# One-hot tiles built one token at a time on VectorE, all low halves on VectorE, and 88 instead of 68 expert chunks prepared during routing

## The chip, the cores and the metric

The kernel runs on one core of one Trainium2 chip. The metric is the device time of one execution in microseconds (us). Engines are named as in the profile: PE is TensorE (matmuls), PEld its weight loads, DVE is VectorE, ACT is ScalarE, POOL is GpSimd, SP is SyncE, which here only issues DMAs.

## What is computed

A decoder trunk of 2 layers for one sequence of 512 tokens and width 1024. Each layer has a mixer (RWKV-7 heads and a pooling mixer) and a PEER expert layer; both are preceded by an RMSNorm with shift and scale from a conditioning vector. The change touches the expert layer most. Cut to what matters, it is:

```python
def peer_ffn(h, peer_q, peer_keys, peer_u, peer_v):        # 8 heads, 128 x 128 experts
    q = (h @ peer_q).reshape(B, S, 8, 2, 128)
    scores = einsum('bshpd,hpkd->bshpk', q, peer_keys)       # 128 keys a half
    s, i = top_k(scores, 16)
    cand_s = s[..., 0, :, None] + s[..., 1, None, :]         # 16 x 16 candidates
    cand_i = i[..., 0, :, None] * 128 + i[..., 1, None, :]
    top_s, sel = top_k(cand_s, 16)
    idx = take_along_axis(cand_i, sel); gate = softmax(top_s)
    # per token: 8 * 16 = 128 chosen experts
    act = gelu(einsum('td,ted->te', hx, peer_u[idx]))
    out = einsum('te,ted->td', gate * act, peer_v[idx])
```

## The kernel before

**Two ways to the same sum.** The 512 tokens are 4 tiles of 128. Tile 0 goes the sparse way: its 128 chosen rows of `peer_u` and of `peer_v` are fetched by indirect DMAs (`gather_load`, issued on POOL, 512 KB each for the 128 tokens) and used on DVE (`gather_use`: line 873 for a u row, line 881 for a v row). The 384 tokens of tiles 1 to 3 go the dense way: all 16384 experts in 128 chunks of 128. A chunk's *first product* (`s_chunk`) is 24 matmuls of 128x384, h times the chunk of `peer_u`. After a Gelu it is multiplied with a gate matrix G (zero where an expert was not chosen). Its *second product* (`back`) is 18 matmuls of 128x512 with the chunk of `peer_v`, summed in PSUM.

**Products in three parts.** For accuracy in fp32r every f32 operand is split in a high half (ACT rounds it: line 265 for weights, line 1156 for v) and a low half (what remains, a subtraction). The low half of a weight tile (`wsp`, 128x1024, line 266) is made on POOL for every second tile of the list `seq`, on DVE for the others (`on_pool`); some tiles of the mixer's `w_in` always go to POOL. The low halves of v (`vv`, two of 128x512 a chunk, line 1157) are made one on DVE and one on POOL.

**The stages of a layer.** (1) Mixer. (2) Queries: 16 tiles of 24 matmuls, each followed by scores and a top-16 on DVE (`score`); meanwhile pieces of the next modulation vector are summed (`ada_acc`: with `side=ND` ACT scales and POOL adds). (3) Routing: for each token tile the candidates are built, sorted and picked on DVE, with one multiply of 128x400 on POOL (lines 981 and 983). For tiles 1 to 3 the gate matrix is built by one-hots: for each of 48 blocks of `TB` = 8 tokens, `onehot` writes tiles with a 1 at (token's expert row i, column j), two of them weighted with the gate's high and low part, and `onehot_mm` turns them into G with 16 matmuls of 128x128 in f16 (a weight load and a matmul for each token and part). G goes to a DRAM scratch. In between, `s_ahead` computes the first products of the first `SPILL` chunks and stores their Gelu in DRAM. (4) Dense: for chunk c, `front` reads the stored Gelu back (c < SPILL) or computes the first product there and then, multiplies with G (line 1145) and splits the result (lines 1147, 1148); `values` splits v; `back` multiplies; `gathers` loads and uses the rows of tile 0.

**What sets the order.** Routing steps and first products are interleaved by `blend` with a weight for each step (`WC`, `WP`, `WG`, `WT`, and `WO` for a one-hot block). `upto(c)` says how many gathered rows are loaded by chunk c: 24 in routing, 0.9 a chunk up to SPILL, and the rest evenly over the chunks from SPILL to 123. The framework then schedules all instructions by estimated times and fixes each engine's order; at run time every engine works its list in that order and waits by semaphores.

## Time and profile before

| | |
|---|---|
| time, three runs | 3843.79, 3853.39, 3864.01 us (median 3853.39) |
| profiled execution, from first to last instruction | 3864.3 us |
| busy in it: PE, DVE, POOL, ACT | 3636.7 us (94%), 3061.0 (79%), 2206.7 (57%), 1494.1 (39%) |
| granted TensorE clock, mean | 0.91 of full speed |
| DMA | 810.70 MB, 210 GB/s over the span |

Busy time is the time in which at least one instruction of the engine was under way. A matmul's end is modelled, so a busy PE is not a PE at its peak. [...] The stages of layer 0 lie at 0 to 467 us (mixer), 467 to 597 (queries), 597 to 1115 (routing), 1121 to 1392 (dense, chunks whose first product was stored) and 1392 to 1920 (dense, the other 60); those of layer 1 at 1947, 2367, 2485, 3006 and 3273 us.

### The profile page before, as it was taken

What the parts mean: (1) busy time and instruction counts of PE and PEld (TensorE: products, weight loads), DVE (VectorE), ACT (ScalarE), POOL (GpSimd) and SP (SyncE); (2) the same over time, 40 slices, a digit from 0 to 9 for tenths busy, and PEclk for the clock granted to TensorE, in tenths of its full rate; (3) what the DMA queues carried; (4) which work ended last, traced back from release to release, by engine and by line L of the source; (5) the groups of instructions that cost most, each with busy time, mean ns of one, the idle gap of its engine ahead of it and who ended that gap; (6) DMA issues with size and microseconds to landing.
All of it is one profiled execution on the core that took longest, in us unless ns stands there. A gap on an engine that the chain in (4) does not pass through costs nothing. (4 is left out here: it accounts for less than half of the span.)

```text
span 3864.3 us, 51554 instructions
## 1 busy us (share of the span) xinstructions
PE 3636.7 (94%) x18154; PEld 3097.8 (80%) x18154; DVE 3061.0 (79%) x5457; ACT 1494.1 (39%) x2361; POOL 2206.7 (57%) x1440
## 2 busy tenths in 40 slices
PE   5999898899999999999998999999999999999998
PEld 4787688778788888888776877887888888888887
DVE  4765489988659999999848456999886798778888
ACT  4443263344443333333353424334344433333333
POOL 3532285656446677887627204366554566767765
PEclk7886799889789999999988789998887999999999
DMA  5223253455469999999713224245554899889885
GB/s 180 77 67 103 93 186 119 159 181 179 154 227 336 340 338 322 330 331 330 265 60 93 66 77 143 90 141 177 179 170 174 308 340 336 286 303 315 308 297 214
DMA packets 349859, 810.70 MB, mean 210 GB/s; under 512 B 45216, under 2 KB 178080, under 8 KB 346272
## 3 DMA queue, kind: packets, MB, share of 16 engines
q1 hardware_dynamic: 275872, 538.94, 41.5%
q0 software_dynamic: 73728, 268.47, 19.3%
q8 instruction: 142, 2.33, 0.2%
q14 instruction: 117, 0.96, 0.1%
HBM read 722.89 MB, written 84.41 MB: 209 GB/s over the span
## 5 line engine op out<-in xcount | busy, mean ns | idle before, releaser
L283 PE MATMUL pss<-hi,wsp 128*128 128x384 f32 (+1 forms) x5168 | 1148.0, 378 | 47.5 <-DVE wsp L266 15.7
L1174 PE MATMUL ps<-vv,wg 128*128 128x512 f32 x4608 | 1098.8, 396 | 58.9 <-ACT wg L1147 29.7
L283 PEld LDWEIGHTS pss<-hi,wsp 128*128 128x128 f32 x5168 | 1021.1, 208 | 120.4 <-DVE wsp L266 17.9
L1174 PEld LDWEIGHTS ps<-vv,wg 128*128 128x128 f32 x4608 | 867.7, 190 | 257.3 <-ACT wg L1147 38.5
L266 POOL TENSOR_TENSOR wsp<-raw,wsp 128x1024 fp32r<-128x1024 f32 x185 | 479.1, 2590 | 439.6 <-ACT wsp L265 420.3
L1157 POOL TENSOR_TENSOR vv<-raw,vv 128x512 fp32r<-128x512 f32 x256 | 387.2, 1513 | 369.5 <-ACT vv L1156 347.0
L265 ACT ACTIVATE wsp<-raw 128x1024 fp32r<-128x1024 f32 x341 | 359.8, 1057 | 587.4 <-PE pss L283 397.6
L283 PE MATMUL pss<-lo,wsp 128*128 128x384 f32 (+1 forms) x2584 | 534.9, 348 | 0.0
L283 PEld LDWEIGHTS pss<-lo,wsp 128*128 128x128 f32 x2584 | 463.7, 189 | 21.9 <-issue 0.5
L873 DVE SCALAR_TENSOR_TENSOR row<-row,hx 128x1024 f32<-128x1024 f32 x256 | 426.3, 1670 | 33.0 <-DMA row<-u,ex 32.8
L881 DVE SCALAR_TENSOR_TENSOR ox<-row,wx,ox 128x1024 f32<-128x1024 f32 x254 | 420.0, 1654 | 15.4 <-DMA row<-v,ex 11.7
L1156 ACT ACTIVATE vv<-raw 128x512 fp32r<-128x512 f32 x512 | 293.7, 621 | 255.2 <-DMA raw<-v 227.4
L1055 PE MATMUL ps<-oh,oh 128*128 128x128 f16 x1536 | 374.7, 414 | 5.5 <-DVE oh L1038 5.5
L867 POOL DMA_INDIRECT row<-v,ex x256 | 339.4, 1326 | 66.3 <-issue 47.7
L1147 ACT ACTIVATE wg<-ge 128x384 fp32r<-128x384 f32 x256 | 132.3, 522 | 617.6 <-DVE ge L1145 506.7
L867 POOL DMA_INDIRECT row<-u,ex x256 | 338.0, 1320 | 50.2 <-issue 32.5
L1036 POOL TENSOR_TENSOR oh<-oh,selg 128x1024 f16<-128x1024 f16 x96 | 208.4, 2173 | 266.2 <-PE ps L1055 252.8
L1055 PEld LDWEIGHTS <-oh 128*128 128x128 f16 x1536 | 217.1, 146 | 136.8 <-issue 9.7
L1157 DVE TENSOR_TENSOR vv<-raw,vv 128x512 fp32r<-128x512 f32 x256 | 254.1, 993 | 61.1 <-ACT vv L1156 61.0
L1145 DVE TENSOR_TENSOR ge<-ge,g 128x192 f32<-128x192 f32 x496 | 245.6, 532 | 28.1 <-DMA g<-gscr 18.3
L1057 ACT ACTIVATE gb<-ps 128x512 f32<-128x512 f32 x192 | 213.2, 1111 | 122.7 <-PE ps L1055 120.5
L266 DVE TENSOR_TENSOR wsp<-raw,wsp 128x1024 fp32r<-128x1024 f32 x156 | 219.9, 1410 | 38.0 <-ACT wsp L265 37.1
(459 smaller groups left out, 4102.8 us busy)
## 6 DMA issues: line engine op xcount, KB each, us to landing
raw<-uT SPq DMA_DIRECT2D x256, 512.0 KB
raw<-v SPq DMA_DIRECT2D x256, 512.0 KB
gscr<-gb SPq DMA_DIRECT2D x24, 2048.0 KB
g<-gscr SPq DMA_DIRECT2D x124, 384.0 KB
gespill<-ge SPq DMA_DIRECT2D x136, 192.0 KB
ge<-gespill SPq DMA_DIRECT2D x136, 192.0 KB
ada<-ada SPq DMA_DIRECT2D x96, 256.0 KB
raw<-ada SPq DMA_DIRECT2D x48, 512.0 KB
```

Source lines behind the costliest of these rows:

```text
L265: S.activation(w[:, 0], raw, AF.Copy)
L266: (G if on_pool(i) else V).tensor_tensor(w[:, 1], raw, w[:, 0].bitcast(F32), op=ALU.subtract)
L283: TE.matmul(pt, w[:, a, k * P:(k + 1) * P], hs[k][b], start=start and n == 0, stop=stop and n == len(steps) - 1)
L867: G.indirect_dma_start(out=rows[n], out_offset=None, in_=A["u" if n < P else "v"], in_offset=bass.IndirectOffsetOnAxis(ap=ex[:, n % P:n % ...
L873: V.scalar_tensor_tensor(row, row, 1.0, hx, op0=ALU.mult, op1=ALU.mult, accum_out=dots[:, e:e + 1])
L881: V.scalar_tensor_tensor(ox, row, wx[:, e:e + 1], ox, op0=ALU.mult, op1=ALU.add)
L1055: TE.matmul(pt[:, tt], oj[:, :, t4 * 4 + tt], xg[:, :, t4 * 4 + tt], start=(q == 0), stop=(q == 1))
L1057: S.activation(gb[:, :, o:o + 4].rearrange("p i t -> p t i"), pt, AF.Copy, scale=1.0 / GSC)
L1145: V.tensor_tensor(gq, gq, g[:, :, c % IG], op=ALU.mult)
L1156: S.activation(vv[0][q], raw[:, q * T:(q + 1) * T], AF.Copy)
L1157: vlo[q] = (V, G)[q].tensor_tensor(vv[1][q], raw[:, q * T:(q + 1) * T], vv[0][q].bitcast(F32), op=ALU.subtract)
L1174: end[0] = TE.matmul(acc[t][d2], wg[a][:, ts_], vv[b][d2], start=(c == 0 and a == 0 and b == 0), stop=(c == NK - 1 and a == 1))
```

## The change

It does eight things. (1) The one-hot tiles are no longer made for 8 tokens by one instruction each over 128x1024 (three on DVE, one on POOL), but token by token, by three `tensor_scalar` of 128x128 in f16 on DVE, with the token's index and gate as scalars read per partition. (2) Their layout changes from (key, token) to (token, key), so that what a matmul reads for one token lies side by side. (3) `iot`, the row of key numbers, shrinks to 128 columns. (4) `on_pool` gives every low half of a weight tile to DVE, but for the named `w_in` tiles. (5) Both low halves of v go to DVE. (6) `ada_acc` in the query stage runs on DVE alone. (7) `SPILL` is 88 instead of 68, `WO` 2.6 instead of 1.9. (8) A chunk's row loads are no longer ordered behind the low half of v.

```diff
-SPILL = 68
+SPILL = 88
-WC, WP, WG, WT, WO = 3.0, 2.8, 3.0, 1.0, 1.9
+WC, WP, WG, WT, WO = 3.0, 2.8, 3.0, 1.0, 2.6
     def on_pool(i):
-        if seq[i][0][:4] == "w_in" and seq[i][1] in SIDE:
-            return True
-        return i % 2 == 0
+        return seq[i][0][:4] == "w_in" and seq[i][1] in SIDE
...
-                iot = rt.tile([P, NK, TB], F16, name="iot")
-                G.tensor_copy(iot, C("iota").unsqueeze(2).to_broadcast([P, NK, TB]))
+                iot = rt.tile([P, NK], F16, name="iot")
+                V.tensor_copy(iot, C("iota"))
...
                 def onehot(b):
-                    V.tensor_tensor(oi, iot, bc("i"), op=ALU.is_equal)
-                    pace["G"] = G.tensor_tensor(x2, oi, bc("g2"), op=ALU.mult)
-                    V.tensor_tensor(x1, oi, bc("g1"), op=ALU.mult)
-                    pace["V"] = V.tensor_tensor(oj, iot, bc("j"), op=ALU.is_equal)
+                    for k in range(TB):
+                        at = lambda n: sel[n][:, b * TB + k:b * TB + k + 1]
+                        V.tensor_scalar(oj[:, k], iot, at("j"), None, op0=ALU.is_equal)
+                        V.tensor_scalar(x1[:, k], iot, at("i"), at("g1"), op0=ALU.is_equal, op1=ALU.mult)
+                        pace["V"] = V.tensor_scalar(x2[:, k], iot, at("i"), at("g2"), op0=ALU.is_equal, op1=ALU.mult)
...
-                                TE.matmul(pt[:, tt], oj[:, :, t4 * 4 + tt], xg[:, :, t4 * 4 + tt], start=(q == 0), stop=(q == 1))
+                                TE.matmul(pt[:, tt], oj[:, t4 * 4 + tt], xg[:, t4 * 4 + tt], start=(q == 0), stop=(q == 1))
...
-                            adas.append((hp, *pre[0], ada_acc(*pre.pop(0), side=ND, early=True)))
+                            adas.append((hp, *pre[0], ada_acc(*pre.pop(0), early=True)))
...
-                    vlo[q] = (V, G)[q].tensor_tensor(vv[1][q], raw[:, q * T:(q + 1) * T], vv[0][q].bitcast(F32), op=ALU.subtract)
+                    vlo[q] = V.tensor_tensor(vv[1][q], raw[:, q * T:(q + 1) * T], vv[0][q].bitcast(F32), op=ALU.subtract)
...
             def gathers(c, vlo):
-                with tc.issue_after(vlo[1].ins):
-                    for n in range(upto(c - 1), upto(c)):
-                        gather_load(n)
+                for n in range(upto(c - 1), upto(c)):
+                    gather_load(n)
```

Most lines of the changed kernel carry a number that is 2 to 7 lower than before (line 266 becomes 264, 881 becomes 879, 1055 becomes 1049, 1157 becomes 1151). Three places show how the order moves.

DVE late in routing, before: a block is three instructions (1035, 1037, 1038; `oh` are the one-hot tiles, `seli`, `selj` and `selg` the tokens' indices and gates), with a weight's low half and a gathered row between blocks.

```order
L1035 TENSOR_TENSOR oh_5639<-iot,seli 128x1024
L1035 TENSOR_TENSOR oh_5643<-iot,seli 128x1024
L1037 TENSOR_TENSOR oh_5636<-oh_5635,selg_3285 128x1024
L1038 TENSOR_TENSOR oh_5634<-iot,selj 128x1024
L873 SCALAR_TENSOR_TENSOR row_8136,dots<-row_8136,hx 128x1024
L266 TENSOR_TENSOR wsp_8332<-raw_8330,wsp_8332 128x1024
L1037 TENSOR_TENSOR oh_5640<-oh_5639,selg_3285 128x1024
L1038 TENSOR_TENSOR oh_5638<-iot,selj 128x1024
```

The same place of the change: the end of a run of 24 small instructions, then the low half of a weight (line 264), a gathered row, and the next run.

```order
L1030 TENSOR_SCALAR oh_5661<-iot,selj 128x128
L1031 TENSOR_SCALAR oh_5662<-iot,seli,selg_3285 128x128
L1032 TENSOR_SCALAR oh_5663<-iot,seli,selg_3286 128x128
L264 TENSOR_TENSOR wsp_9783<-raw_9781,wsp_9783 128x1024
L871 SCALAR_TENSOR_TENSOR row_9343,dots<-row_9343,hx 128x1024
L1030 TENSOR_SCALAR oh_5664<-iot,selj 128x128
L1031 TENSOR_SCALAR oh_5665<-iot,seli,selg_3285 128x128
```

So a block on DVE grew from three instructions to 24, and the low halves of weights between the blocks doubled.

PE late in routing, before: the last weight load and matmul of 16 for a block, and then a first product (`pss`) to its end before the next block's 16 begin.

```order
L1055 LDWEIGHTS oh_5638
L1055 MATMUL ps_8612<-oh_5641,oh_5638 128x128
L283 MATMUL pss_8628<-hi_3236,wsp_8475 128x384 x2
L283 MATMUL pss_8628<-hi_3241,wsp_8475 128x384 x2
...
L283 MATMUL pss_8628<-lo_3267,wsp_8475 128x384
L283 MATMUL pss_8628<-lo_3272,wsp_8475 128x384
L1055 LDWEIGHTS oh_5642
L1055 MATMUL ps_8661<-oh_5644,oh_5642 128x128
```

The same place of the change, within one first product.

```order
L281 MATMUL pss_10233<-lo_3257,wsp_10029 128x384
L1049 LDWEIGHTS oh_5664
L1049 MATMUL ps_10163<-oh_5665,oh_5664 128x128
L281 MATMUL pss_10233<-lo_3262,wsp_10029 128x384
L1049 LDWEIGHTS oh_5664
L1049 MATMUL ps_10163<-oh_5666,oh_5664 128x128
L281 MATMUL pss_10233<-lo_3267,wsp_10029 128x384
```

Single one-hot matmuls now stand between the matmuls of a first product, token by token as DVE's order yields them, and each is a place where PE can wait for DVE.

POOL in the second part of the dense stage, before: row loads between low halves of v and of weights.

```order
L867 DMA row_27490<-v,ex 128x1024
L1157 TENSOR_TENSOR vv_23846<-raw_27514,vv_23844 128x512
L867 DMA row_27559<-v,ex 128x1024
L867 DMA row_27561<-v,ex 128x1024
L867 DMA row_27563<-v,ex 128x1024
L266 TENSOR_TENSOR wsp_27451<-raw_27449,wsp_27451 128x1024
L1157 TENSOR_TENSOR vv_23850<-raw_27586,vv_23848 128x512
L867 DMA row_27627<-v,ex 128x1024
```

In the change POOL's list has row loads alone here. What left it stands on DVE, where about one chunk of this part reads so (1151 makes the low halves of v, 1139 multiplies with G, 1142 makes the low half of the result, 264 that of a weight, 879 uses a row).

```order
L879 SCALAR_TENSOR_TENSOR ox<-row_15063,wx,ox 128x1024
L879 SCALAR_TENSOR_TENSOR ox<-row_15065,wx,ox 128x1024
L1151 TENSOR_TENSOR vv_10430<-raw_15167,vv_10428 128x512
L1151 TENSOR_TENSOR vv_10431<-raw_15167,vv_10429 128x512
L879 SCALAR_TENSOR_TENSOR ox<-row_15067,wx,ox 128x1024
L1139 TENSOR_TENSOR ge_9901<-ge_9901,g_15024 128x192
L1139 TENSOR_TENSOR ge_9901<-ge_9901,g_15026 128x192
L879 SCALAR_TENSOR_TENSOR ox<-row_15069,wx,ox 128x1024
L1142 TENSOR_TENSOR wg_10417<-ge_9901,wg_10416 128x384
L264 TENSOR_TENSOR wsp_15175<-raw_15173,wsp_15175 128x1024
```

Here DVE has both low halves of v and one low half of a weight in every chunk, where it had one of v and, in every second chunk, one of a weight.

## Rows read from the trace of the kernel before

**Rows 1.** Busy time by stage: stretch and its length in us, then busy us (and instructions) of PE, its weight loads, DVE, ACT and POOL, the granted clock, the DMA engines' busy share, GB/s. The stages of layer 0 are queries, routing until the first one-hot, the rest of routing, and the two parts of dense; then of layer 1 the queries, routing in one, and the second part of dense (without its last 40 us).

```profile
467.00:597.00 130.00, 123.22 (x624) 105.55 (x624) 112.79 (x585) 73.38 (x111) 83.56 (x59) 0.95 0.51 175
597.00:693.00 96.00, 80.89 (x431) 79.46 (x432) 89.07 (x304) 30.56 (x42) 57.06 (x41) 0.91 0.47 141
693.00:1115.00 422.00, 410.72 (x1886) 341.44 (x1885) 340.76 (x491) 175.83 (x195) 244.89 (x128) 0.85 0.50 170
1121.00:1392.00 271.00, 269.46 (x1193) 224.41 (x1192) 247.19 (x370) 104.14 (x200) 169.13 (x122) 0.99 0.96 333
1392.00:1920.00 528.00, 511.27 (x2537) 457.15 (x2537) 483.52 (x507) 189.26 (x310) 414.58 (x269) 0.99 0.90 320
...
2367.00:2485.00 118.00, 114.23 (x582) 97.72 (x580) 109.98 (x589) 50.53 (x75) 44.06 (x31) 0.98 0.35 115
2485.00:3006.00 521.00, 502.36 (x2342) 429.27 (x2343) 434.74 (x787) 211.60 (x241) 298.71 (x169) 0.85 0.49 163
...
3273.00:3820.00 547.00, 510.26 (x2471) 451.75 (x2470) 461.64 (x495) 178.34 (x299) 397.12 (x265) 0.98 0.86 304
```

**Rows 2.** The costliest group of PE and the costliest of DVE from 700 to 1115 us: line, engine, operation, tiles, form, count, then busy us, mean ns of one, and the idle time before them with what ended it.

```profile
L1055 PE MATMUL ps<-oh,oh 128*128 128x128 f16 x744 | 181.7, 414 | 5.5 <-DVE oh L1038 5.5
...
L1038 DVE TENSOR_TENSOR oh<-iot,selj 128x1024 f16<-128x1024 f16 x47 | 87.2, 1856 | 0.0
L1037 DVE TENSOR_TENSOR oh<-oh,selg 128x1024 f16<-128x1024 f16 x47 | 51.2, 1090 | 71.9 <-PE ps L1055 71.9
L1035 DVE TENSOR_TENSOR oh<-iot,seli 128x1024 f16<-128x1024 f16 x47 | 49.8, 1071 | 0.0
L873 DVE SCALAR_TENSOR_TENSOR row<-row,hx 128x1024 f32<-128x1024 f32 x24 | 46.1, 1922 | 2.8 <-DMA row<-u,ex 2.8
L266 DVE TENSOR_TENSOR wsp<-raw,wsp 128x1024 fp32r<-128x1024 f32 x24 | 38.6, 1607 | 5.0 <-ACT wsp L265 5.0
```

**Rows 3.** PE in order of time in the middle of routing: start us, length us, engine, line, operation, count.

```profile
843.56 3.92 PE L1055 MATMUL ps<-oh,oh 128*128 128x128 f16 x16
847.13 3.15 PE L283 MATMUL pss<-hi,wsp 128*128 128x384 f32 x16
850.11 1.55 PE L283 MATMUL pss<-lo,wsp 128*128 128x384 f32 x8
851.50 3.93 PE L1055 MATMUL ps<-oh,oh 128*128 128x128 f16 x16
855.07 4.60 PE L283 MATMUL pss<-hi,wsp 128*128 128x384 f32 x16
```

**Rows 4.** The same view in the query stage: 8 matmuls of 128x128 in f32, whose operands lie side by side, and what follows.

```profile
497.67 1.05 PE L935 MATMUL ps<-keys,qT 128*128 128x128 f32 x8
498.48 1.85 PE L283 MATMUL pss<-hi,wsp 128*128 128x512 f32 x7
```

**Rows 5.** Single lines of DVE over the whole run: count, shortest, median and longest duration in ns, first and last start.

```profile
L196 DVE TENSOR_SCALAR acc<-raw,silu_c x6: 472/481/482, 277.0 to 2270.0; 128x512 f32<-128x512 f32 x6
L879 DVE TENSOR_SCALAR ox<-row,wx x2: 742/748/753, 1541.1 to 3438.0; 128x1024 f32<-128x1024 f32 x2
L1038 DVE TENSOR_TENSOR oh<-iot,selj x96: 675/2380/6514, 694.0 to 2987.9; 128x1024 f16<-128x1024 f16 x96
L266 DVE TENSOR_TENSOR wsp<-raw,wsp x156: 1194/1215/3348, 40.5 to 3816.3; 128x1024 fp32r<-128x1024 f32 x156
L1157 DVE TENSOR_TENSOR vv<-raw,vv x256: 676/684/4598, 1128.2 to 3839.0; 128x512 fp32r<-128x512 f32 x128
L198 DVE SCALAR_TENSOR_TENSOR acc<-raw,silu_c,acc x42: 736/747/753, 279.0 to 2278.4; 128x512 f32<-128x512 f32 x42
L881 DVE SCALAR_TENSOR_TENSOR ox<-row,wx,ox x254: 1270/1285/5240, 1546.1 to 3825.0; 128x1024 f32<-128x1024 f32 x127
L1148 DVE TENSOR_TENSOR wg<-ge,wg x256: 543/552/2757, 1127.6 to 3843.7; 128x384 fp32r<-128x384 f32 x128
```

**Rows 6.** DVE, POOL and PE in order of time in the second part of the dense stage.

```profile
1500.22 4.28 PE L1174 MATMUL ps<-vv,wg 128*128 128x512 f32 x18
1500.24 1.23 POOL L867 DMA_INDIRECT row<-u,ex  x1
1500.56 1.21 DVE L873 SCALAR_TENSOR_TENSOR row<-row,hx 128x1024 f32<-128x1024 f32 x1
1501.70 0.62 DVE L1145 TENSOR_TENSOR ge<-ge,g 128x192 f32<-128x192 f32 x2
1504.06 4.80 DVE L873 SCALAR_TENSOR_TENSOR row<-row,hx 128x1024 f32<-128x1024 f32 x1 [1.74 <-DMA row<-u,ex]
1504.13 2.40 POOL L266 TENSOR_TENSOR wsp<-raw,wsp 128x1024 fp32r<-128x1024 f32 x1
1504.34 2.96 PE L283 MATMUL pss<-hi,wsp 128*128 128x384 f32 x16
1506.48 1.29 POOL L1157 TENSOR_TENSOR vv<-raw,vv 128x512 fp32r<-128x512 f32 x1
```

**Rows 7.** DMA issues by line: tiles, queue, count, KB each.

```profile
raw<-uT SPq DMA_DIRECT2D x256, 512.0 KB
raw<-v SPq DMA_DIRECT2D x256, 512.0 KB
g<-gscr SPq DMA_DIRECT2D x124, 384.0 KB
```

More of the change, by code (lines that the diff above doesn't have):

```diff
@@ L1027, in onehot @@
                     if not ohr:
-                        ohr.extend([[s2t("oh", (P, NK, TB), F16) for _ in range(4)] for _ in range(3)])
-                    oj, oi, x1, x2 = ohr[b % 3]
-                    t0 = b * TB
-                    def bc(n):
-                        return sel[n][:, t0:t0 + TB].unsqueeze(1).to_broadcast([P, NK, TB])
-                    V.tensor_tensor(oi, iot, bc("i"), op=ALU.is_equal)
-                    pace["G"] = G.tensor_tensor(x2, oi, bc("g2"), op=ALU.mult)
-                    V.tensor_tensor(x1, oi, bc("g1"), op=ALU.mult)
-                    pace["V"] = V.tensor_tensor(oj, iot, bc("j"), op=ALU.is_equal)
+                        ohr.extend([[s2t("oh", (P, TB, NK), F16) for _ in range(3)] for _ in range(3)])
+                    oj, x1, x2 = ohr[b % 3]
+                    for k in range(TB):
[3 more added lines that the diff above has]
+                        pace["V"] = V.tensor_scalar(x2[:, k], iot, at("i"), at("g2"), op0=ALU.is_equal, op1=ALU.mult)
                     onehot_mm()
@@ L1045, in onehot_mm @@
                     b = pend.pop()
-                    oj, oi, x1, x2 = ohr[b % 3]
+                    oj, x1, x2 = ohr[b % 3]
                     t0 = b * TB
```

## The prediction

> **What bounds the kernel now.** I read the busy time by stage first, then the costliest groups of routing, then single stretches in order of time.
>
> In the dense stage PE sets the pace. It is busy for 269 of 271 us in the first part and 511 of 528 in the second, at a granted clock of 0.99 [rows 1]. A stored chunk costs 271/68 = 3.99 us; its 18 matmuls last 4.28, and the next group starts 4.12 after them [rows 6]. A chunk with its first product costs 528/60 = 8.8 us in layer 0 and 547/60 = 9.1 in layer 1, where 4.12 + 4.3 = 8.4 would do: 24 matmuls of a first product hold PE for 4.37 us from 847.13 to 851.50 [rows 3], where the first 16 last 3.15; in dense they last 2.96 [rows 6]. The DMA engines are 0.96 and 0.90 busy, so nothing is far below PE.
>
> Routing is two things. Until the first one-hot DVE is the busiest (89 of 96 us). After it PE is busy for 411 of 422 us, at a clock of 0.85, and DVE waits for it: 71.9 us ahead of line 1037 alone [rows 1, 2]. PE's largest group there is not the first products but the one-hot matmuls, 181.7 us for 744. Sixteen of them hold PE for 3.57 us (from 843.56 to 847.13), 223 ns each for 128 columns [rows 3]. The chunk behind such a run starts slow: its first 16 matmuls take 4.60 us in one case, 3.15 in another. So the one-hots cost PE their own time and some of the clock. Eight f32 matmuls of the same size, whose operands lie side by side, hold PE for 0.81 us, 101 ns each [rows 4].
>
> **What POOL does to DVE.** A use of a row takes 1.21 us beside an indirect load, but 4.80 us beside two subtractions on POOL (2.40 and 1.29) [rows 6]. Line 1038 is at best 0.675 us, but 2.38 in the median [rows 5]. So DVE's busy time holds waits for POOL's arithmetic, none of which I see beside loads. The change takes nearly all that arithmetic away but the 400-column multiply of routing.
> [...]
>
> **The new one-hots on DVE.** No row shows a 128-column f16 `tensor_scalar` with per-partition scalars. The nearest are line 196 (512 columns f32, 481 ns) and line 879 (1024, 748) [rows 5]: 0.52 ns a column and 214 ns fixed. At that slope 128 columns take 281 ns. Should f16 halve the slope, as between lines 266 and 1038 (1.19 to 0.675 us), it is 247. At the rate of a subtraction, 1.04 ns a column (lines 266 and 1157: 1215 less 684 for 512 columns), it is 347. Neighbours overlap by about 0.08 us: two of line 1145 take 0.62 [rows 6], those of 384 columns 0.55 each [rows 5], which makes 0.35 for 192. So an instruction costs 0.17, 0.20 or 0.27 us. Two of three have a second scalar; a first one costs 63 ns (line 198 against 1157, both 512 columns), which would add 0.04 on the mean. I take 0.20, and keep 0.17 to 0.31. A block is 24 of them, 4.8 us, where before it was 192/48 = 4.0 us of DVE with POOL's stretch (188.2 us for 47 [rows 2]).
> [...]
>
> **Routing after the change.** By the weights (32.2, 29.4 and, with `WO` 2.6, 183.6), 22 chunks fall before the first one-hot and 66 behind it; now 20 and 48.
> - DVE behind it: 340.8 busy less 192 for one-hots is 149. Stretch that goes: 24 rows by 0.7 (1.92 to 1.22) and 24 low halves by 0.4, 26 in all. Low halves: 66 in place of 24, 42 by 1.14 = 48. That is 171, and 1152 instructions by 0.20 = 230, in all 401. DVE at its fullest is 0.93 busy (89 of 96), so 401/0.93 = 431.
> - PE behind it: 66 by 4.3 = 284, and 48 by 16 by 101 ns = 78, in all 362. DVE is the later.
> So 431 in place of 422, and 5 more for two chunks and 12 low halves ahead of the first one-hot: **+15 us a layer**, with 18 more chunks done than before.
>
> **Dense after the change.** Twenty chunks go from 8.8 to 4.0 us: 96 us a layer in layer 0 and 102 in layer 1. What is lost is in the 36 chunks behind them that carry rows: `upto` now spreads 153 rows over 36 chunks, 4.25 each, where it was 171 over 56, 3.05. Per such chunk:
> - DVE: 4.25 by 1.285, two of line 1145 at 0.35, 0.55, two of 0.684 and 1.215, less 0.08 for each of 10: 8.5 us, with no arithmetic left on POOL.
> - PE: 8.4.
> - DMA: uT, v and 4.25 rows at 512 KB, and 192 KB of G (384 KB twice for four chunks) [rows 7]: 3.47 MB. At the 333 GB/s of the first part, with the engines 0.96 busy, up to 347: 10.0 us. But these engines' busy time also holds waits of their own, so this is an upper bound.
> I take 9.5, between 8.5 and 10.0. The loss is 36 by 0.7 = 25 in layer 0, 36 by 0.4 = 14 in layer 1. The first part keeps its pace: DVE there has 0.9 rows, 3.3 us for a 4.0 us chunk. Saved: 71 and 88, on the mean **75 to 80 a layer**; I count 75.
>
> **Queries and the rest.** Six `ada_acc` in layer 0 (two in layer 1) give DVE 8 instructions each, 0.48 and seven by 0.747: 5.7 us, 34 in layer 0. Eight more low halves are 10. Against that stand some 18 us of stretch, so 113 busy become about 139 for 130 us of stage: +12, and +2 in layer 1. The mixer's moved low halves (some 13) are hidden by its chains; at worst 13 by 1.2 = 16 us. Row loads that are free of line 1157 only start earlier; they wait for free buffers anyway, and I count nothing.
>
> **Sum.** 2 x (15 - 75) + 14 = -106 us on the profiled execution's 3864, that is 3758; this execution is 0.3% above the median of 3853, so **3750**.
>
> **Rivals.**
> 1. *DVE falls behind in routing, slower than before.* Place: the runs of 24 `tensor_scalar`; PE's one-hot matmuls stand inside first products and wait for them, token by token. Each 0.01 us an instruction costs 11.5/0.93 = 12.4 us a layer. From 0.243 us on the gain is gone; at 0.31 routing grows by 136 more a layer, 4020 in all. For: every scalar row has a large fixed part. Against: line 196 has such a scalar and still takes half the time of a subtraction for each column. Chance 0.19.
> 2. *The row loads bind.* At 10.0 us or a little more a chunk dense saves 53 and 70: 3780 or so. For: 0.96 busy in the first part. Against: that part still ran at PE's pace. Chance 0.13.
> 3. *Routing shrinks.* At 0.17 us DVE needs 367/0.93 = 394, PE 362 at full clock: 37 less a layer, and with dense at 9.0 us a chunk 18 more: 3640. For: no f16 pattern with a stride is left, and the clock no longer falls behind a run of one-hots. Against: PE has gaps while it waits for DVE. Chance 0.18.
> 4. *POOL and the one-hots hold each other up*, as POOL's arithmetic holds up line 873 [rows 6]. Behind the first one-hot POOL has 32 multiplies of 400 columns (0.94 us each by the 2.40 of 1024) and 24 row loads (1.23): up to 60 us a layer, half of it likely, 3750 + 60 = 3810. For: the 4.80 us. [...] Chance 0.07. [...]
>
> **Chances.** My forecast 0.43 (3690 to 3820). Half a per cent, 19 us, is what a measurement can tell from no change. Slower by more: rival 1's upper part, 0.15, and 0.02 of others. Same: 0.06, mostly where an instruction costs about 0.24 us. Faster: 0.77. The range takes rivals 2 to 4 and the lower part of the first: 3640 to 3880.
>
> **What will show it.** Right: `tensor_scalar` near 0.25 us long and 0.2 apart; the one-hot matmuls at 100 ns or less; DVE about 0.93 busy in routing, no longer waiting for PE; DVE lines in dense at their shortest durations; dense chunks of 4.0 and 9 to 9.5 us. Wrong: routing over 560 us, with PE idle ahead of one-hot matmuls; or waits of DVE for rows in dense, with POOL late.

## The result and the profile after

The changed kernel takes 3695.76 us (median of four runs, 3694.2 to 3716.36) where the kernel before took 3855.03 beside it. The ratio is 0.9587, with a 95% interval of 0.9554 to 0.9621: 159 us or 4.1% less. The profiled execution has a span of 3694.9 us, against 3864.3.

The first lines of its page (busy us, share of the span, instructions):

```profile
span 3694.9 us, 53159 instructions
PE 3383.4 (92%) x18154; PEld 2930.2 (79%) x18154; DVE 3017.8 (82%) x7953; ACT 1425.0 (39%) x2295; POOL 1094.6 (30%) x872
```

DVE has eight times the instructions per block and nearly all the low halves, and yet is busy for 3018 us where it was busy for 3061. POOL fell from 2207 to 1095, PE from 3637 to 3383.

Busy time by stage, columns as in [rows 1]: for layer 0 the queries, routing until the one-hots, the rest of routing (cut at 710 us, 7 us behind the first one-hot), and the two parts of dense; for layer 1 the queries, routing in one, and the two parts of dense.

```profile
456.00:593.00 137.00, 121.29 (x575) 101.00 (x576) 127.16 (x568) 40.42 (x61) 3.93 (x8) 0.90 0.49 162
593.00:710.00 117.00, 104.17 (x575) 101.46 (x574) 108.76 (x418) 39.06 (x52) 45.24 (x33) 0.96 0.51 144
710.00:1126.00 416.00, 370.44 (x2326) 339.40 (x2324) 401.91 (x1512) 190.12 (x232) 69.25 (x55) 0.91 0.59 200
1134.00:1480.00 346.00, 345.02 (x1524) 285.49 (x1523) 279.34 (x573) 135.44 (x258) 92.27 (x81) 1.00 0.99 348
1480.00:1856.00 376.00, 357.07 (x1757) 314.92 (x1755) 339.66 (x458) 130.69 (x227) 199.98 (x157) 0.98 0.95 354
2282.00:2406.00 124.00, 116.75 (x577) 98.67 (x578) 113.73 (x574) 40.47 (x62) 3.82 (x8) 0.94 0.35 113
2406.00:2937.00 531.00, 464.20 (x2871) 433.95 (x2869) 502.01 (x1885) 229.81 (x283) 106.82 (x88) 0.92 0.56 188
2943.00:3320.00 377.00, 372.08 (x1657) 308.61 (x1657) 298.68 (x603) 148.74 (x284) 99.27 (x86) 0.99 0.97 338
3320.00:3680.00 360.00, 342.00 (x1665) 303.25 (x1663) 318.53 (x418) 118.45 (x200) 199.64 (x150) 0.98 0.94 344
```

Behind the first one-hot the bound has changed hands: PE had 411 busy us of 422 [rows 1], now it has 370 of 416, and DVE has 402 of 416. Routing is as long as before, with 20 more first products in it, some 18 of them in this stretch. The gain stands in dense.

The table gives the same for all kernels of this study: us over both layers for the queries (from the norm ahead of them to the last matmul of the scores), for routing (from there to the first second product), for dense, and for the rest (mixers, what is left of a layer's rows, the end), all from the profiled execution; these bounds are not those of the stretches above. A chunk's pace is the mean distance between the starts of the second products of neighbouring chunks, layer 0 / layer 1; "stored" chunks read their Gelu back (from chunk 4 to chunk SPILL - 2), "computed" ones make their first product there (from SPILL + 1 to 123).

| kernel | median us | queries | routing | dense | rest | stored chunk | computed chunk |
|---|---|---|---|---|---|---|---|
| before | 3855 | 239 | 1081 | 1646 | 898 | 4.11 / 4.17 | 8.66 / 9.28 |
| low_only | 3792 | 247 | 1087 | 1569 | 898 | 4.14 / 4.26 | 8.35 / 8.38 |
| onehot_only | 3864 | 238 | 1063 | 1656 | 898 | 4.15 / 4.23 | 8.87 / 9.27 |
| spill88_only | 3944 | 239 | 1247 | 1542 | 914 | 4.14 / 4.19 | 10.10 / 9.90 |
| onehot_spill88 | 3872 | 238 | 1144 | 1570 | 913 | 4.15 / 4.50 | 10.08 / 10.11 |
| after_spill68 | 3756 | 261 | 1016 | 1587 | 897 | 4.12 / 4.25 | 8.52 / 8.51 |
| **changed** | 3696 | 261 | 1078 | 1459 | 897 | 4.10 / 4.20 | 8.88 / 9.11 |
| after_v_pool | 3728 | 257 | 1075 | 1494 | 896 | 4.16 / 4.18 | 9.52 / 9.17 |
| after_strided | 3924 | 259 | 1311 | 1464 | 898 | 4.08 / 4.24 | 9.27 / 8.96 |
| after_g_twice | 3785 | 259 | 1077 | 1551 | 893 | 4.75 / 4.79 | 8.73 / 8.96 |
| after_one_scalar | 3646 | 261 | 1024 | 1451 | 905 | 4.11 / 4.19 | 8.99 / 8.91 |
| after_ada_pool | 3665 | 249 | 1070 | 1457 | 889 | 4.10 / 4.24 | 9.06 / 9.04 |
| after_spill100_ada | 3728 | 247 | 1135 | 1347 | 998 | 4.10 / 4.14 | 9.46 / 8.82 |
| ada_act_x2b | 3615 | 246 | 1010 | 1466 | 895 | 4.12 / 4.21 | 8.99 / 9.21 |

So the change of 169 us between the two profiled executions is, rounded, -187 in dense, -3 in routing, +21 in the queries, and -1 in the rest.

The costliest groups from 710 to 1126 us, columns as in [rows 2]:

```profile
L281 PE MATMUL pss<-hi,wsp 128*128 128x384 f32 x1041 | 229.4, 374 | 26.2 <-ACT ge L852 20.1 <-DVE wsp L264 6.1
...
L1031 DVE TENSOR_SCALAR oh<-iot,seli,selg 128x128 f16<-128x128 f16 x376 | 120.1, 320 | 7.1 <-PE ps L1049 7.1
L1032 DVE TENSOR_SCALAR oh<-iot,seli,selg 128x128 f16<-128x128 f16 x376 | 119.5, 318 | 0.0
...
L1030 DVE TENSOR_SCALAR oh<-iot,selj 128x128 f16<-128x128 f16 x376 | 96.3, 256 | 0.0
...
L264 DVE TENSOR_TENSOR wsp<-raw,wsp 128x1024 fp32r<-128x1024 f32 x65 | 81.7, 1258 | 2.2 <-ACT wsp L263 2.1
L1049 PE MATMUL ps<-oh,oh 128*128 128x128 f16 x763 | 77.1, 225 | 17.3 <-DVE oh L1031 12.3 <-DVE oh L1030 2.3 <-DVE oh L1032 0.8
```

The one-hot matmuls (line 1049) fell from 181.7 to 77.1 us [rows 2]. DVE waited 71.9 us for them and now waits 7.1; PE waits for DVE instead, 15.4 of the 17.3 us that it is idle ahead of line 1049.

PE in order of time in the middle of routing, to be read beside [rows 3]:

```profile
903.21 1.55 PE L281 MATMUL pss<-lo,wsp 128*128 128x384 f32 x8
904.60 1.46 PE L1049 MATMUL ps<-oh,oh 128*128 128x128 f16 x23
906.52 0.43 PE L1049 MATMUL ps<-oh,oh 128*128 128x128 f16 x2 [0.46 <-DVE oh L1031]
907.12 0.44 PE L1049 MATMUL ps<-oh,oh 128*128 128x128 f16 x2 [0.17 <-DVE oh L1031]
...
908.88 3.51 PE L281 MATMUL pss<-hi,wsp 128*128 128x384 f32 x10
```

With tiles ready, 23 one-hot matmuls go by in 1.46 us, 63 ns each, where 16 took 3.57 before [rows 3]; the granted clock is 1.00 in both places (843.5 to 847.1 us before, 904.6 to 906.06 now). In both traces it is recorded at either 1.00 or 0.50, so 0.91 over a stretch is a mean of the two. Then PE has caught up with DVE, and two come every 0.60 us, DVE's pace for one token.

Single lines of DVE over the whole run, columns as in [rows 5]:

```profile
L1031 DVE TENSOR_SCALAR oh<-iot,seli,selg x768: 284/304/1000, 705.8 to 2935.7; 128x128 f16<-128x128 f16 x192
L1030 DVE TENSOR_SCALAR oh<-iot,selj x768: 223/244/1018, 703.1 to 2935.5; 128x128 f16<-128x128 f16 x192
L879 DVE SCALAR_TENSOR_TENSOR ox<-row,wx,ox x254: 1268/1279/1296, 1554.3 to 3669.0; 128x1024 f32<-128x1024 f32 x127
L1151 DVE TENSOR_TENSOR vv<-raw,vv x512: 676/685/3056, 1131.2 to 3668.4; 128x512 fp32r<-128x512 f32 x171
```

The use of a v row (line 879, before 881) never takes longer than 1.296 us now; before it took up to 5.24 [rows 5]. The 3.056 us of line 1151 is a single instruction, at 1837 us, beside a MEMSET of 3.5 us on POOL.

### The profile page after: what moved, and what is told of

The parts are those of the page before. It is cut to its first block, busy times and chain, and to the rows that moved or that the text cites. A ratio compares the mean times of both kernels' runs of the same rounds, so it can differ in the third digit from the quotient of the medians.

```text
span 3694.9 us, 53159 instructions
## 1 busy us (share of the span) xinstructions
PE 3383.4 (92%) x18154; PEld 2930.2 (79%) x18154; DVE 3017.8 (82%) x7953; ACT 1425.0 (39%) x2295; POOL 1094.6 (30%) x872
## 5 line engine op out<-in xcount | busy, mean ns | idle before, releaser
L281 PEld LDWEIGHTS pss<-hi,wsp 128*128 128x128 f32 x5168 | 987.0, 203 | 188.9 <-ACT ge L852 63.2
L264 DVE TENSOR_TENSOR wsp<-raw,wsp 128x1024 fp32r<-128x1024 f32 x314 | 397.8, 1268 | 43.3 <-ACT wsp L263 42.4
L1151 DVE TENSOR_TENSOR vv<-raw,vv 128x512 fp32r<-128x512 f32 x512 | 344.7, 690 | 46.3 <-ACT vv L1150 44.6
L981 POOL TENSOR_TENSOR eq<-eq,cid 128x400 f32<-128x400 f32 x128 | 166.9, 1323 | 623.6 <-DVE eq L979 585.0
L879 DVE SCALAR_TENSOR_TENSOR ox<-row,wx,ox 128x1024 f32<-128x1024 f32 x254 | 325.0, 1280 | 3.0 <-DMA row<-v,ex 0.4
L871 DVE SCALAR_TENSOR_TENSOR row<-row,hx 128x1024 f32<-128x1024 f32 x256 | 315.0, 1237 | 10.1 <-DMA row<-u,ex 9.9
L1031 DVE TENSOR_SCALAR oh<-iot,seli,selg 128x128 f16<-128x128 f16 x768 | 243.2, 318 | 10.2 <-PE ps L1049 10.2
L1032 DVE TENSOR_SCALAR oh<-iot,seli,selg 128x128 f16<-128x128 f16 x768 | 242.8, 318 | 0.1
L1142 DVE TENSOR_TENSOR wg<-ge,wg 128x384 fp32r<-128x384 f32 x256 | 140.6, 554 | 102.8 <-ACT wg L1141 85.7
L1030 DVE TENSOR_SCALAR oh<-iot,selj 128x128 f16<-128x128 f16 x768 | 194.7, 255 | 2.2 <-PE ps L1049 2.2
L1139 DVE TENSOR_TENSOR ge<-ge,g 128x192 f32<-128x192 f32 x496 | 156.0, 352 | 42.4 <-DMA g<-gscr 28.1
```

Of the source, the lines that this page charges most:

```text
L264: (G if on_pool(i) else V).tensor_tensor(w[:, 1], raw, w[:, 0].bitcast(F32), op=ALU.subtract)
L281: TE.matmul(pt, w[:, a, k * P:(k + 1) * P], hs[k][b], start=start and n == 0, stop=stop and n == len(steps) - 1)
L871: V.scalar_tensor_tensor(row, row, 1.0, hx, op0=ALU.mult, op1=ALU.mult, accum_out=dots[:, e:e + 1])
L879: V.scalar_tensor_tensor(ox, row, wx[:, e:e + 1], ox, op0=ALU.mult, op1=ALU.add)
L1030: V.tensor_scalar(oj[:, k], iot, at("j"), None, op0=ALU.is_equal)
L1031: V.tensor_scalar(x1[:, k], iot, at("i"), at("g1"), op0=ALU.is_equal, op1=ALU.mult)
```

## The experiments

Two theories stood at first. **Theory 1**: the gain is 20 first products a layer moved out of dense into a routing that has room once the one-hots cost PE less; the low halves only make room. **Theory 2**: the gain is DVE freed of POOL's arithmetic. Theory 3, the layout on PE alone, was a third.

### One part alone

`low_only`: all low halves on DVE, rows not ordered behind them, nothing else.

```diff
-        if seq[i][0][:4] == "w_in" and seq[i][1] in SIDE:
-            return True
-        return i % 2 == 0
+        return seq[i][0][:4] == "w_in" and seq[i][1] in SIDE
...
-                    vlo[q] = (V, G)[q].tensor_tensor(...)
+                    vlo[q] = V.tensor_tensor(...)
...
-                with tc.issue_after(vlo[1].ins):
-                    for n in range(upto(c - 1), upto(c)):
-                        gather_load(n)
+                for n in range(upto(c - 1), upto(c)):
+                    gather_load(n)
```

> The kernel before with parts 4, 5 and 8 of the change alone: all low halves on VectorE, row loads free of them; one-hots, SPILL and WO as before. Theory 1 (the gain comes from 20 first products a layer that routing takes over, and the rest only makes room for them): routing stays bound by PE (411 of 422 us busy before), so nothing there; a dense chunk with its first product falls from 9.1 to about 8.6 us, 60 times, at most 30 us a layer: 3800 to 3840 us. Theory 2 (the gain is VectorE freed of POOL's arithmetic): most of the 160 us stay without the other parts, 3700 to 3750 us.

Measured: 3792.12 us, ratio 0.9819 (0.9793 to 0.9844). Busy time behind the first one-hot and in the second part of dense, layer 0, columns as in [rows 1]:

```profile
704.00:1126.00 422.00, 412.57 (x1867) 341.94 (x1866) 315.53 (x498) 176.84 (x194) 178.88 (x103) 0.83 0.49 169
...
1398.00:1914.00 516.00, 516.00 (x2602) 466.41 (x2600) 431.59 (x618) 193.66 (x332) 226.01 (x175) 1.00 0.91 327
```

DVE has more instructions and less busy time than in the kernel before, in routing 316 us for 341. PE holds routing as it did, 413 of 422, so there the freed DVE buys nothing; in dense PE now runs without a gap, and the computed chunk falls to 8.35 us, further than the 8.6 of theory 1. The time lies between the two theories, 8 us below the first's range and 42 above the second's.

`onehot_only`: the one-hots and their layout alone (the second, third and fourth piece of the diff in the section on the change).

> The kernel before with parts 1 to 3 alone: one-hots token by token and their new layout; low halves, SPILL 68 and WO 1.9 as before. Theory 1: PE loses 105 us a layer in routing (181.7 us of one-hot matmuls before, 77.1 after), but VectorE becomes the bound at 341 - 192 + 1152 x 0.20 = 379 us busy, 0.95 of some 400 us: 15 to 30 us a layer, 3795 to 3825 us. Theory 3 (the layout on PE is the gain by itself): routing falls by the 105 us of PE, 3645 us.

Measured: 3864.27 us, ratio 1.0012 (0.9995 to 1.0029): no difference. Theory 1 and theory 3 both miss. The stretch of one-hots in layer 0:

```profile
697.00:1110.00 413.00, 324.04 (x1927) 273.86 (x1924) 408.26 (x1480) 166.33 (x196) 124.26 (x78) 0.86 0.51 173
```

PE has only 324 busy us of 413, but DVE has 408. Theory 1 had counted 379 for it. What it left out is the next section's: POOL's subtractions hold up a run of small instructions too (line 1033 takes 0.301 us in the median and up to 3.181 here).

`spill88_only`: 88 chunks and `WO` 2.6 alone.

```diff
-SPILL = 68
+SPILL = 88
-WC, WP, WG, WT, WO = 3.0, 2.8, 3.0, 1.0, 1.9
+WC, WP, WG, WT, WO = 3.0, 2.8, 3.0, 1.0, 2.6
```

> The kernel before with part 7 alone: SPILL 88 and WO 2.6. Theory 1: routing is bound by PE, so 20 first products of 4.3 us add about 86 us a layer there, and dense gives back 20 x 5 = 100 us less what the denser row loads cost (14 to 25): within 25 us of before, 3840 to 3885 us. Rival (the shift is worth as much by itself, since routing had room): 3700 us.

Measured: 3943.99 us, ratio 1.0226 (1.0197 to 1.0256), slower, and 59 us above theory 1's range. The same two stretches:

```profile
706.00:1200.00 494.00, 491.05 (x2289) 420.78 (x2289) 344.58 (x484) 202.90 (x230) 256.03 (x135) 0.89 0.50 170
...
1554.00:1982.00 428.00, 376.34 (x1753) 327.87 (x1752) 391.65 (x393) 130.31 (x220) 326.08 (x223) 0.94 0.90 318
```

Routing is PE's throughout (491 of 494) and grows by 83 us a layer, as theory 1 said (86). What it missed is dense, which gives back only 52 a layer, not 75 to 86: with 4.25 rows a chunk and half of the low halves on POOL, a computed chunk takes 10.1 and 9.9 us, with PE busy for 0.88 of it. The shift by itself is a loss, and its price is in both stages.

### Two parts of three

`onehot_spill88`: the changed kernel with the low halves as before. Part 6, which the text on record does not name, is undone in it as well: its queries are those of before.

> The changed kernel with the low halves as before (half of the weights' and half of v's on POOL, rows loaded behind v's): parts 4, 5 and 8 undone. Theory 1: routing as in the changed kernel or 10 us a layer shorter, dense 15 to 30 us a layer longer, since VectorE is stretched beside POOL's subtractions again: 3705 to 3760 us. Theory 2 (freed VectorE is the gain): 3800 us or more.

Measured: 3872.10 us, ratio 1.0043 (1.0024 to 1.0061). Theory 1 misses by more than 110 us, theory 2's bound holds: without free low halves nothing is left of the gain. Against the changed kernel routing is 66 us longer and dense 111, over both layers. Parts 4, 5 and 8 alone part this kernel from `after_ada_pool` below, which takes 3665.36 us: with all else the same, they are worth 207 us here. One one-hot line over the whole run, columns as in [rows 5], and DVE and POOL in order of time in routing:

```profile
L1033 DVE TENSOR_SCALAR oh<-iot,seli,selg x768: 286/301/3092, 697.7 to 3042.4; 128x128 f16<-128x128 f16 x192
```

```profile
1042.57 0.35 DVE L1034 TENSOR_SCALAR oh<-iot,seli,selg 128x128 f16<-128x128 f16 x1
1042.79 2.58 DVE L1032 TENSOR_SCALAR oh<-iot,selj 128x128 f16<-128x128 f16 x1
1042.89 2.41 POOL L266 TENSOR_TENSOR wsp<-raw,wsp 128x1024 fp32r<-128x1024 f32 x1
...
1045.29 0.30 DVE L1033 TENSOR_SCALAR oh<-iot,seli,selg 128x128 f16<-128x128 f16 x1
```

An instruction of 0.24 us takes 2.58 because POOL starts a subtraction of 2.41 us beside it; it ends 0.07 us behind POOL's. Of line 1033's 768 instructions the median is at its normal 301 ns, the longest at ten times that. The trace has 27 stalls above 1.5 us behind the first one-hot of layer 0, each beside one of POOL's subtractions, and of the 2304 one-hot instructions of both layers none begins and ends within such a subtraction. The three one-hot lines are busy there for 146.5, 136.6 and 113.1 us, 396 in all, where the changed kernel has 336; so DVE is busy for 439 us in place of 402 although POOL does 33 of its subtractions.

`after_spill68`: the changed kernel with `SPILL = 68` (`WO` stays at 2.6).

> The changed kernel with SPILL back at 68. Theory 1: dense loses 50 to 85 us a layer, routing gains about 20 (18 low halves and 18 ACT roundings fewer behind the first one-hot, VectorE the bound): 3760 to 3825 us. Theory 2 (freed VectorE): no more than 10 us from the changed kernel, 3700 us.

Measured: 3756.40 us, ratio 0.9728 (0.9705 to 0.9752), 4 us below theory 1's range and 60 above the changed kernel. Moving the 20 chunks costs routing 31 us a layer, 1.5 us a chunk where PE needs 4.3, and gives dense 64. That is what "room" is worth: PE is busy for 323 of 397 us behind the first one-hot at 68, and for 370 of 416 at 88.

```profile
705.00:1102.00 397.00, 322.71 (x1996) 282.55 (x1992) 384.61 (x1497) 169.19 (x203) 67.96 (x55) 0.88 0.54 184
```

`after_v_pool`: the changed kernel, with one of the two low halves of v on POOL again.

```diff
-                    vlo[q] = V.tensor_tensor(...)
+                    vlo[q] = (V, G)[q].tensor_tensor(...)
```

> The changed kernel with part 5 undone: the second low half of every v chunk on POOL again, all else as changed. It parts the 50 to 61 us a layer that dense lost when parts 4, 5 and 8 were undone together. Theory (POOL's subtraction of each chunk stretches VectorE, 1.3 us by 128 chunks, and only weights' low halves matter in routing): dense 25 to 50 us a layer longer, routing unchanged, 3745 to 3795 us. Rival (the weights' low halves of the last 40 chunks, 2.4 us each on POOL, did it, or part 8's order): 3720 us or less.

Measured: 3728.45 us, ratio 0.9671 (0.9634 to 0.9709). Dense is 35 us longer over both layers, where theory had 25 to 50 for each, and routing is as before; the time lies between the theory's and the rival's. So v's low halves by themselves are some 35 of the 111 us that dense lost in `onehot_spill88`; the rest lies with the weights' low halves on POOL, with the order of the row loads, or with these coming together, which no run parts.

### The layout on PE

`after_strided`: the changed kernel, with the matmuls reading its tiles at the old stride.

```diff
+                turn = lambda z: z.rearrange("p a b -> p (a b)").rearrange("p (i t) -> p i t", t=TB)
...
-  TE.matmul(pt[:, tt], oj[:, t4 * 4 + tt], xg[:, t4 * 4 + tt], ...)
+  TE.matmul(pt[:, tt], turn(oj)[:, :, t4 * 4 + tt], turn(xg)[:, :, t4 * 4 + tt], ...)
```

> The changed kernel, but the one-hot matmuls read the same tiles with the old stride (elements of one column 8 apart), which makes another gate matrix and has each matmul wait for the whole block. Theory 1 (layout sets PE's price): a one-hot matmul goes back from 0.10 to 0.22 us, 768 of them add 95 to 110 us a layer to PE's 370, which passes VectorE's 402: routing 60 to 110 us a layer longer, 3810 to 3900 us. Rival (VectorE binds anyway and PE has room): 3700 to 3720 us.

Measured: 3923.75 us, ratio 1.0178 (1.0143 to 1.0212), slower than before by 68 us and 24 us above theory 1's range. The one-hot matmuls behind the first one-hot of layer 0 (columns as in [rows 2]), and the stretch itself:

```profile
L1051 PE MATMUL ps<-oh,oh 128*128 128x128 f16 x768 | 188.6, 414 | 3.0 <-DVE oh L1031 2.9
```

```profile
710.00:1240.00 530.00, 505.06 (x2339) 429.27 (x2339) 410.05 (x1523) 205.11 (x234) 68.11 (x55) 0.86 0.46 158
```

The stride brings back the 181.7 us of [rows 2] (188.6 for all 768), for the same instructions of DVE. Routing grows by 116 us a layer, more than the 60 to 110 expected: PE is busy for 135 us more in this stretch; the one-hot matmuls take 112 more, and at a granted clock of 0.86 in place of 0.91 the first products grow too (their matmuls with `hi`: 248 us for 229). The wait for a whole block shows as 3 us of PE's idle time, so the difference between 189 and 77 us is the stride; dense is within 6 us of the changed kernel.

### What holds the changed kernel now

`after_one_scalar`: the third one-hot tile without its second scalar.

```diff
-  pace["V"] = V.tensor_scalar(x2[:, k], iot, at("i"), at("g2"), op0=ALU.is_equal, op1=ALU.mult)
+  pace["V"] = V.tensor_scalar(x2[:, k], iot, at("i"), None, op0=ALU.is_equal)
```

> The changed kernel with the third one-hot tile (x2) made by one comparison, without its second scalar; the gate's low part is left out of the product, so the output differs. Theory (VectorE is what routing waits for, 402 of 416 us busy, and a second scalar costs 0.06 us): 384 x 0.06 = 23 us a layer less, 3640 to 3660 us. Rival (routing is held by the mesh of waits between PE, ACT and VectorE, and 0.97 busy is a coincidence): 3685 us or more.

Measured: 3645.96 us, ratio 0.9455 (0.942 to 0.949). The stretch of one-hots in layer 0:

```profile
710.00:1106.00 396.00, 356.74 (x2363) 330.32 (x2364) 388.13 (x1519) 195.73 (x243) 71.78 (x55) 0.95 0.63 216
```

Routing falls by 27 us a layer for 23 us of DVE, which is still busy for 388 of 396: DVE is what routing waits for.

`after_g_twice`: every load of G in dense done a second time, into a tile that nobody reads.

```diff
                         nc.sync.dma_start(g8[q], gd[q * NG // 2:(q + 1) * NG // 2, :, c:c + IG].rearrange(...))
+                        gx8 = dp.tile([P, NG // 2, IG, GB], F32, tag="gx8", name=nm("gx8"), bufs=2)
+                        nc.sync.dma_start(gx8, gd[q * NG // 2:(q + 1) * NG // 2, :, c:c + IG].rearrange(...))
```

> The changed kernel with each load of the gate matrix in dense done a second time into a tile that nobody reads: 192 KB a chunk more. Theory A (a DMA busy share of 0.95 to 0.99 means full): 192 KB at 350 GB/s is 0.55 us a chunk, 124 chunks, 68 us a layer: 3800 to 3840 us. Theory B (the engines' busy time holds waits of their own, and they move more when asked, as the 384 GB/s of one slice says): stored chunks stay at PE's 3.9 us, and only the 40 others pay up to 0.5 us: 3700 to 3745 us.

Measured: 3784.90 us, ratio 0.981 (0.977 to 0.9849), 89 us above the changed kernel and between the ranges of the two theories. Stretches of layer 0 with stored chunks and with computed chunks, and ACT's rounding of v in the stored part, here and (line 1150) in the changed kernel from 1134 to 1480 us (columns as in [rows 1] and [rows 2]):

```profile
1134.00:1535.00 401.00, 360.33 (x1510) 288.65 (x1510) 276.28 (x566) 134.53 (x253) 89.70 (x79) 0.97 1.08 359
...
1700.00:1850.00 150.00, 147.49 (x737) 131.11 (x736) 145.57 (x175) 51.84 (x86) 85.81 (x70) 1.00 1.02 388
```

```profile
L1152 ACT ACTIVATE vv<-raw 128x512 fp32r<-128x512 f32 x166 | 94.8, 621 | 99.7 <-DMA raw<-v 97.1 <-PE ps L1169 2.4
...
L1150 ACT ACTIVATE vv<-raw 128x512 fp32r<-128x512 f32 x169 | 95.6, 619 | 34.3 <-DMA raw<-v 25.2 <-PE ps L1167 8.2 <-issue 0.5
```

Each theory holds in one part. Stored chunks go from 4.10 to 4.75 us: ACT waits 97 us for v in place of 25, and the rate rises only from 348 to 359 GB/s. So among stored chunks the loads were close to the most that this run gets, at the same time as PE was busy throughout. What sets the 359 is not shown: SP waits 18 us, from 1134 to 1480 us, for the landing of the added loads themselves before it issues the next ones, so a part of the delay can come from the edit and not from full DMA engines. Computed chunks do not grow (8.73 for 8.88 us): the additional bytes are hidden, at 388 GB/s, where the changed kernel moves up to 381 (1650 to 1800 us). The busy share, 1.02 to 1.08, does not tell these cases apart.

### Versions that go further

`after_ada_pool`: part 6 undone, the sums of `ada_acc` in the queries on ACT and POOL again.

```diff
-  adas.append((hp, *pre[0], ada_acc(*pre.pop(0), early=True)))
+  adas.append((hp, *pre[0], ada_acc(*pre.pop(0), side=ND, early=True)))
```

> The changed kernel with part 6 undone: the sums of ada_acc in the queries on ACT and POOL again. Theory: the 15.5 and 5.9 us that the query stages grew are VectorE's extra 8 instructions for each sum, so they go back to about 125 and 119 us: 3675 to 3685 us. Rival: POOL's adds slow VectorE by as much as they take off it: 3696 us, no difference.

Measured: 3665.36 us, ratio 0.9518 (0.9476 to 0.9561). That is 30 us below the changed kernel, more than expected. In the profiles 12 us of it lie in the queries, 8 in routing and 8 in the rest. Why routing and the rest follow isn't settled: kernels with the same mixer code differ by up to 17 us in the stretch of layer 1's mixer (415.7 to 432.8 us).

`after_spill100_ada`: that kernel with `SPILL = 100`.

> The changed kernel with part 6 undone and SPILL 100. If routing still has room as in the changed kernel: dense loses another 12 x 4.5 us a layer, routing gains 12 x 1.2 (VectorE) and the queries 12 and 4 back: 3600 to 3640 us. If routing is full (VectorE 402 of 416 us, PE 370) or the row loads, now within 24 chunks, bind: 3680 us or more.

Measured: 3727.80 us, ratio 0.9678 (0.9643 to 0.9713), 62 us above `after_ada_pool`; of the two expectations the second came. Against `after_ada_pool` dense falls by another 110 us, as expected, but routing grows by 65 where 29 were expected, 2.7 us a chunk, and the rest grows by 109. The 58 us behind the last second product of layer 0 and the 65 behind that of layer 1, and the uses of v rows (line 879) in each:

```profile
1832.00:1890.00 58.00, 17.91 (x83) 16.60 (x82) 44.94 (x63) 10.14 (x36) 30.59 (x27) 0.53 0.68 249
...
3662.00:3727.00 65.00, 0.00 (x0) 0.00 (x0) 49.42 (x55) 8.13 (x21) 33.76 (x28) 0.52 0.64 238
```

```profile
L879 DVE SCALAR_TENSOR_TENSOR ox<-row,wx,ox 128x1024 f32<-128x1024 f32 x27 | 34.7, 1285 | 4.8 <-DMA row<-v,ex 4.0
...
L879 DVE SCALAR_TENSOR_TENSOR ox<-row,wx,ox 128x1024 f32<-128x1024 f32 x28 | 36.0, 1284 | 6.1 <-DMA row<-v,ex 5.3
```

PE has 18 us of work in the first stretch and none in the second, while DVE uses the last 27 and 28 rows of v. With 24 computed chunks instead of 36 there are 5.9 row loads for each, and not all the uses fit beside the chunks; whether DVE or the loads keep them out was not parted.

`ada_act_x2b`: part 6 undone, and the one-hots spread over DVE and ACT.

```diff
-  V.tensor_scalar(x1[:, k], iot, at("i"), at("g1"), op0=ALU.is_equal, op1=ALU.mult)
-  pace["V"] = V.tensor_scalar(x2[:, k], iot, at("i"), at("g2"), op0=ALU.is_equal, op1=ALU.mult)
+  V.tensor_scalar(oi[:, k], iot, at("i"), None, op0=ALU.is_equal)
+  pace["V"] = V.tensor_scalar(x1[:, k], oi[:, k], at("g1"), None, op0=ALU.mult)
+  S.activation(x2[:, k], oi[:, k], AF.Copy, scale=at("g2"))
```

> The changed kernel with part 6 undone (3665 us), and with the one-hots spread over two engines: VectorE makes oj, a plain one-hot oi and x1 = oi x g1, each with one scalar, and ACT makes x2 = oi x g2 (g2 kept in f32 for it). VectorE: 384 x (0.61 - 0.49) = 46 us a layer less, of which the run with one scalar in x2 showed 28 for 23; ACT: 384 x up to 0.30 (its shortest 128-column lines) = 115 us more on 192 of 414. Theory: routing falls until PE (365 us busy) is the bound, some 30 us a layer: 3590 to 3620 us. Rival (ACT's list delays the weights' high halves and the Gelus that PE waits for): 3665 us or more.

Measured: 3614.76 us, ratio 0.938 (0.9343 to 0.9417), the fastest of this study, 81 us below the changed kernel. Behind the first one-hot of layer 0, and ACT's new line there:

```profile
700.00:1085.00 385.00, 345.58 (x2326) 325.05 (x2325) 358.68 (x1510) 290.13 (x613) 71.86 (x55) 0.93 0.63 217
```

```profile
L1033 ACT ACTIVATE oh<-oh,selg 128x128 f16<-128x128 f16 x383 | 129.2, 424 | 17.8 <-DVE oh L1031 16.8
```

From the first one-hot to the last, layer 0 takes 392 us in place of the 419 of `after_ada_pool`. In the stretch shown DVE is busy for 359 of 385 us and PE for 346: the two are nearly level, and ACT, at 290, has not become the bound.

## Why the prediction was right

The sign, the place of the gain and the likeliest case held, though near its lower edge of 3690 us; the time came out 54 us lower than forecast and within the range. The two large errors, in routing and in dense, go the same way (33 and 37 us over both layers), so the hit does not rest on errors that cancel. By its steps:

- **Price of a one-hot instruction**, taken as 0.20 us. In rows of the trace it is 0.163 from start to start with one scalar and 0.223 with two, 0.203 on the mean of a token's three. The additional 60 ns for a second scalar is what the pair of lines 198 and 1157 had shown [rows 5]. Of the three figures that the sum chose among, 0.17 is near the form with one scalar; that f16 would halve the slope, which it stood on, was the author's estimate from lines 266 and 1038. Rival 1 needed 0.243 and so did not come.
- **DVE in routing**, 401 us: measured 401.9 from 710 us on, and 408.9 from the first one-hot at 703 us. **PE in routing**, 362: measured 370.4. **The one-hot matmuls**, 101 ns: 77.1 us for 763, the same on the mean. That is partly luck: where tiles wait ready they take 63 ns each, while a pair that waits for DVE is busy for 0.43 us; and the busy times of PE's groups overlap now that they are interleaved (229.4 and 106.1 us of first products and 77.1 of one-hots in 370.4), so only their sum is tested. `after_strided` shows that the layout is the cause of the fall from 181.7.
- **Routing +15 a layer** was too much: it is -3 over both. The mis-sized term is how full DVE can be, taken as 0.93 from the stage ahead of the first one-hot; it is 402 of 416, 0.97. DVE waits for almost nothing there (7.1 us ahead of the one-hots); in the stage from which the 0.93 came it is 0.93 after the change too (109 of 117 us).
- **Dense -75 a layer** was too little: it is -83 and -104. The mis-sized term is the computed chunk, counted at 9.5 us between 8.5 and 10.0; it is 8.88 and 9.11. The upper end stood on a DMA rate of 347 GB/s, taken from the stored chunks. That the engines' busy time there holds more than moving the bytes needs is in the trace of before: from 1121 to 1392 us half of the 15194 packets of 4096 bytes take 159 ns or less, one in a hundred over 580, the longest 2168, and with every packet at the median of its size the busy share would be 0.87 in place of 0.96. Among stored chunks more bytes bring no more than 359 (`after_g_twice`); beside computed chunks the same engines move up to 388. So rival 2 did not come: the rate on which it stood does not carry over from one part of dense to the other. A stored chunk, counted at 4.0 us (271/68), takes 4.10 and 4.20, nearly as before (4.11 and 4.17 in the table).
- **The queries**, +12 and +2: measured 15.5 and 5.9. `after_ada_pool` shows that part 6 is 12 of these 21 us and brings nothing back elsewhere.
- **DVE lines in dense at their shortest durations**: held, [rows 5] against the rows above, but for what lies beside POOL's MEMSETs at 1837 us. The share of the low halves, though, was told too small in theory 1. The sum counted POOL's stretch as 26 us of routing and as a part of a chunk's price; `onehot_spill88` shows that without it nothing of the gain is left. With POOL's subtractions in place the one-hots are held up, which is rival 4's mechanism with another partner.
- **Rival 4** itself, POOL's multiplies of 400 columns and the row loads: of 2304 one-hot instructions 42 lie beside a multiply and take 0.83 to 0.93 us on the mean, some 12 us of DVE a layer. The 160 beside a row load have medians of 0.243 and 0.305, those beside nothing 0.243 and 0.303. On the mean the loads add 0.01 to 0.07 us to an instruction, some 3 us a layer. So both together cost a quarter of the 60 us. That a load could hold DVE up for its whole 1.23 us was the author's estimate, and no run shows it. POOL's arithmetic did hold DVE up for all of its time in `onehot_spill88`: an instruction of 0.24 us took 2.58 beside 2.41 of POOL. Whether the loads wait for DVE in turn, no run here shows.
- **Rival 3**, routing shrinks: not in this kernel. Its condition, a lighter DVE, is what `after_one_scalar` and `ada_act_x2b` meet, and routing then does shrink by 27 to 34 us a layer against the changed kernel. Its other condition came in part: the granted clock in routing rose from 0.85 to 0.91.

Together the runs say that no part carries the gain. Low halves alone bring 67 us (3859 to 3792), the one-hots alone nothing, the 20 chunks alone cost 85. Low halves and one-hots with part 6 bring 103 (3756), and only then the 20 chunks bring 60 more. The one-hots take routing from PE, the low halves keep DVE, which inherits it, from being held up, and the chunks fill the PE time that is then idle. One pair was not run, low halves and chunks without the one-hots. That the chunks need the one-hots too is argued from `low_only`, where PE is busy for 413 of 422 us and has no room for them, and from `spill88_only`, where they cost routing 83 us a layer.

## What to carry to other kernels

When several engines are nearly level in a stage, price a change by the engine that will bound it afterwards, and ask what holds that engine up: here DVE could do its 402 us in 416 because POOL had nearly stopped computing beside it; with POOL's subtractions back it took 439 in 451. Work moved into a stage costs what the bounding engine pays for it (1.5 us a chunk here), not what the moved work takes on its own engine (4.3), and this price need not last: the next 12 chunks cost 2.7 each, with PE busy for 398 of 439 us and DVE for 417. And a DMA rate read in one stage was no bound for another: the changed kernel moved 348 GB/s among stored chunks, at a busy share of 0.99, and up to 381 among computed ones, at 1.01.

## What was not expected of the hardware

- In `onehot_spill88` a DVE instruction of 0.24 us was held for the whole of a POOL subtraction that started beside it: 2.58 us beside 2.41. Small instructions were not let through: none of 2304 began and ended within a subtraction.
- With every load of G doubled, the same 16 DMA engines moved 359 GB/s among stored chunks and 388 among computed ones (1700 to 1850 us), at busy shares of 1.08 and 1.02. Why the first is lower is open.
- A second per-partition scalar costs a `tensor_scalar` of 128x128 60 ns (0.244 to 0.304 us), about what a first one costs a two-input instruction of 512 columns (63 ns, lines 1157 and 198).
- A 128x128 f16 weight load and matmul with elements 16 bytes apart cost PE 223 ns, with elements side by side 63, both at a granted clock of 1.00 in the stretch that was read.
